# Sampled attention stream: one copy per bank of turned weights, exponentials in four portions

## The chip, the cores and the metric

The kernel runs on one core of a Trainium2 chip. A core has a matrix engine, TensorE (PE in the profile), which reads from the on-chip memory SBUF and writes to the accumulator banks of PSUM; VectorE (DVE), ScalarE (ACT) and GpSimd (POOL) for the rest of the arithmetic; and SyncE (SP), which issues most transfers. Each engine runs its own instructions strictly in order and waits for the others by semaphores. The metric is the time of one execution in device microseconds; less is better.

## The reference

The program is one inference step of a one-layer hybrid decoder. Two kinds of rows go through the same weights: a prompt of 2048 new tokens, and 8 sampled sequences of 8 new tokens each with 8192 cached positions. Half of the mixer is attention with forget gates (8 heads of 64), the other half an mLSTM matrix memory (4 heads of 128). An output projection, a layer norm, a squared-ReLU MLP (1024 to 4096 to 1024) and a second layer norm follow. The part that the change touches is the attention of the sampled sequences over their paged cache:

```python
s_past = jnp.einsum('bqhd,bkhd->bhqk', q, k_past).astype(jnp.float32) * scale
s_past = s_past + Ln[..., :, None] + R[:, :, None, :]
...
p = jax.nn.softmax(jnp.concatenate([s_past, s_new], axis=-1), axis=-1).astype(v_new.dtype)
o = jnp.einsum('bhqk,bkhd->bqhd', p[..., :P], v_past) + jnp.einsum('bhqk,bkhd->bqhd', p[..., P:], v_new)
```

All inputs and results are fp32. Large products are made as three products of rounded halves (lines 157 to 159: hi x hi, lo x hi, hi x lo), whose halves ScalarE (line 149, the hi part) and VectorE (line 152, the lo part) make from each weight or activation piece.

## The kernel before, in words

The main line of the program has four stages: A, the input projection with convolution, gates and mLSTM (to about 900 us, tiles `pm`, `whi`, `wlo`); B, the prompt's attention (to about 1325 us); O, the output projection and first norm (to about 1560 us, tiles `pw`, `y`, `px`, `x1h`, `x1l`); and C, the MLP in blocks of rows (tiles `ph`, `hq`, `h`, `py`), each block beginning with norms and transposes of its rows.

Beside it runs the sampled stream, `sample_attention` (line 1856), a generator that the main line advances one step at a time, paced by the estimated time of the matmuls recorded (`tick`, line 129). It has 295 steps n; a sequence b takes 32 of them and its stages overlap with those of the next:

- GpSimd gathers cached keys by indirect DMA into the ring `kT` (line 1996), VectorE turns them (line 2002), TensorE multiplies them with the query (`sQ`, line 2025), and VectorE adds the forget terms and takes running maxima (line 2032). A sequence's 8192 positions leave four pieces `S` (u = 0 to 3), each 128 x 2 x 512.
- At step 35 + 32b, `softmax` finds the maximum over everything (`m4`, line 2057) and ScalarE makes the exponentials in place, eight of 128x512 (line 2062) and two small ones for the new tokens (line 2064), each with its row sums in `rp`.
- At step 37 + 8u', `weights` turns piece u: for each half hg, TensorE makes four 128x128 transposes into one PSUM bank (`sT`, line 2094), which are copied out to `PTs` (line 2096), quarters 0 and 2 by VectorE, 1 and 3 by ScalarE. `sT` and `sQ` and the other small products of the stream share one bank (tag `sX`, one buffer), so the next of them waits until the bank has been emptied. That makes 64 banks of turned weights in all.
- `pv_step` multiplies `PTs` with gathered values (`sO`, line 2137), sixteen times per sequence; step 39 prepares the new tokens' weights (`softmax_new`), step 41 the reciprocal of the row sums (`softmax_sum`), step 70 closes the sequence.

The order on each engine is not the order of the code. The code records instructions; the framework's scheduler then places them by a simulated time line and by what each depends on (`schedule_with_timeline_sim`), and the stream's instructions are only kept behind the last ones of the main line (`beside`, line 114). So a change of one stage moves rows on all engines from there on.

Of the kernel before, what the change touches and what calls it, by code (L numbers as in the profile page):

```python
# [10 lines left out]
F32 = mybir.dt.float32  # L11
F32R = mybir.dt.float32r
I32 = mybir.dt.int32
AF = mybir.ActivationFunctionType
OP = mybir.AluOpType
AX = mybir.AxisListType
# [1839 lines left out]
def sample_attention(tc, I, O, ps_, pps, cst, ident, sqk, dnl, dR, dmix, dqb, vx, kx, pe, ring_a):  # L1856

    nc = tc.nc
    V, A, G, T, SY = nc.vector, nc.scalar, nc.gpsimd, nc.tensor, nc.sync
# [81 lines left out]
    for g in range(2):  # L1941
        p = pps.tile([32, 8, 64], F32, name="sT", tag="sX", bufs=1)
# [16 lines left out]
    state = {}  # L1959
# [9 lines left out]
    def q_load(b):  # L1969
        qt = ps_.tile([128, 2, 16, 8], F32, name="qt", bufs=2)  # L1970
        for n in range(2):
            SY.dma_start(qt[:, n].rearrange("p d t -> p (d t)"), dap(dqb, (n * NB + b) * 4096, [[0, 4], [128, 32], [1, 128]]))
        bn = ps_.tile([128, 2, 8], F32, name="bn", bufs=2)
        for hg in range(2):
            SY.dma_start(bn[:, hg], dap(dnl, hg * 4 * TOT + S + b * 8, [[TOT, 4], [0, 32], [1, 8]]))
        state[b] = dict(qt=qt, bn=bn, U=[])
# [21 lines left out]
    def k_turn(n):  # L1998

        for i in range(2):  # L2000
            x = piece(n)[:, i * 512:(i + 1) * 512]
            V.transpose(x, x)  # L2002
# [34 lines left out]
    def softmax(b):  # L2037
        z = state[b]
        pq = pps.tile([128, 2, 256], F32, name="sQ", tag="sX", bufs=1)
        for hg in range(2):  # L2040
            for db in range(2):
                for h4 in range(4):
                    hd = (hg * 4 + h4) * 2 + db
                    T.matmul(pq[h4 * 32:h4 * 32 + 32, hg, 0:8], z["qb"][:, hd], z["kr"][:, hd],
                             start=(db == 0), stop=(db == 1), skip_group_check=True)
        for hg in range(2):
            V.tensor_tensor_reduce(out=z["Sn"][:, hg], in0=pq[:, hg, 0:8], in1=z["bn"][:, hg], scale=1.0, scalar=NEG,
                                   op0=OP.add, op1=OP.max, accum_out=z["mx"][:, hg, 16:17])

        V.tensor_reduce(mt[:, 0:2], z["mx"], axis=AX.X, op=OP.max)  # L2050
        m2 = ps_.tile([128, 32], F32, name="m2", bufs=2)
        V.transpose(m2, mt)
        m3 = ps_.tile([128, 8], F32, name="m3", bufs=2)
        V.tensor_reduce(m3, m2.rearrange("p (g q) -> p q g", q=8), axis=AX.X, op=OP.max, negate=True)
        V.tensor_copy(m2.rearrange("p (g q) -> p g q", q=8), m3[:, None, :].to_broadcast([128, 4, 8]))
        m4 = ps_.tile([128, 32], F32, name="m4", bufs=2)
        V.transpose(m4, m2)
        rp = z["rp"] = ps_.tile([128, 2, 5], F32, name="rp", bufs=2)
        for u in range(4):
            for hg in range(2):  # L2060
                x = z["U"][u][:, hg].rearrange("p b k t -> p (b k t)")
                A.activation(x, x, AF.Exp, bias=m4[:, hg:hg + 1], accum_out=rp[:, hg, u:u + 1])
        for hg in range(2):
            A.activation(z["Sn"][:, hg], z["Sn"][:, hg], AF.Exp, bias=m4[:, hg:hg + 1], accum_out=rp[:, hg, 4:5])

    def softmax_new(b):

        z = state[b]
        rs = z["rs"] = ps_.tile([128, 2], F32, name="rs", bufs=2)
        V.tensor_reduce(rs, z["rp"], axis=AX.X, op=OP.add)  # L2070
        pn = z["pn"] = ps_.tile([8, 2, 32], F32, name="PTn", bufs=2)
        p = pps.tile([8, 2, 128], F32, name="sT", tag="sX", bufs=1)
        for hg in range(2):
            T.transpose(p[:, hg], z["Sn"][:, hg], ident)
        for hg in range(2):
            A.copy(pn[:, hg].rearrange("p (h q) -> p h q", q=8), p[:, hg].rearrange("p (h g q) -> p g h q", g=4, q=8)[:, 0])

    def softmax_sum(b):
        z = state[b]
        pl = pps.tile([128, 1], F32, name="sT", tag="sX", bufs=1)  # L2080
        for hg in range(2):
            T.matmul(pl, sel[:, hg].rearrange("p a b -> p (a b)"), z["rs"][:, hg:hg + 1], start=(hg == 0), stop=(hg == 1))
        rl = z["rl"] = ps_.tile([128, 1], F32, name="rl", bufs=2)
        V.reciprocal(rl, pl)

    def weights(b, u, hg):

        z = state[b]
        if hg == 0:
            z["PT"] = ps_.tile([128, 2, 4, 4, 4, 8], F32, name="PTs", tag="PTs", bufs=1)  # L2090
        PT = z["PT"]
        p = pps.tile([128, 4, 128], F32, name="sT", tag="sX", bufs=1)
        for f in range(4):
            T.transpose(p[:, f], z["U"][u][:, hg, f].rearrange("p k t -> p (k t)"), ident)
        for f in range(4):
            (A.copy if f % 2 else V.tensor_copy)(PT[:, hg, f].rearrange("p g h q -> p h g q"),
                                                 p[:, f].rearrange("p (h g q) -> p h g q", g=4, q=8))

    def v_new(b):
        vn = state[b]["vn"] = ps_.tile([8, 512], F32, name="vns", bufs=1)  # L2100
        SY.dma_start(vn, O["v_sample"][0, b].rearrange("t h d -> t (h d)"))
# [15 lines left out]
    def v_room():  # L2117
        return kx["free"] and vx["next"] < 128 and len(vx["live"]) < (2 if vx["more"] else 1) and (0 not in vx["live"] or vx["more"])
# [30 lines left out]
    def pv_end(b):  # L2149
        z = state.pop(b)  # L2150
        p = pps.tile([128, 2, 128], F32, name="sT", tag="sX", bufs=1)
        for c in range(2):
            T.transpose(p[:, c], z["os"][:, c * 128:(c + 1) * 128], ident)
        for hh in range(2):
            s = slice(hh * 64, hh * 64 + 64)
            for c in range(2):
                for hg in range(2):
                    V.tensor_reduce(mixs[s, hg * 2 + c, b * 8:b * 8 + 8],
                                    p[s, c].rearrange("p (e g h q) -> p g h q e", e=2, g=2, q=8)[:, hg, 2 * c + hh],
                                    axis=AX.X, op=OP.add)  # L2160

    def at(n, first, of):

        i, r = divmod(n - first, of)
        return i if r == 0 and i >= 0 else None
# [4 lines left out]
    def step(n):  # L2170
        after = None
        if n == 0:
            q_load(0)
        g, r = divmod(n - 2, 4)
        if 0 <= g < GA and r >= 2:
            k_turn(4 * g + 2 * r - 4)
            k_turn(4 * g + 2 * r - 3)
        if NA + 2 < n < 260:
            for i in turns.pop(n, ()):
                k_turn(i)  # L2180
        g = at(n, 6, 4)
        if g is not None and g < 64:
            after = qk_step(g)
        b = at(n, 35, 32)
        if b is not None and b < 8:
            softmax(b)
        due = (n - 38) // 2 if n > NA + 2 else (n - 39) // 2
        lead = 2
        while done[0] < 128 and done[0] - (lead == 1 and done[0] % 2) <= due and got.get(done[0], n) <= n - lead:
            after = pv_step(done[0] // 16, done[0] % 16, after)  # L2190
            done[0] += 1
            lead = 1
        b = at(n, 70, 32)
        if b is not None:
            pv_end(b)
        b = at(n, 39, 32)
        if b is not None and b < 8:
            softmax_new(b)
            v_new(b)
        b = at(n, 41, 32)  # L2200
        if b is not None and b < 8:
            softmax_sum(b)
        u = at(n, 37, 8)
        if u is not None and u < 32:
            for hg in range(2):
                weights(u // 4, u % 4, hg)
        b = at(n, 30, 32)
        if b is not None and b < 7:
            q_load(b + 1)
        b = at(n, 3, 32)  # L2210
        if b is not None and b < 8:
            q_begin(b)
        g = at(n, 4, 4)
        if g is not None and g < 64:
            r_load(g)
        if n >= 35 and (n % 2 == 1 or not vx["live"]):
            while v_room():
                got[vx["next"]] = n
                v_gather()
        g, r = divmod(n - 2, 4)  # L2220
        if 0 <= g < GA and r < 2:
            k_gather(4 * g + 2 * r, r == 1)
            k_gather(4 * g + 2 * r + 1, r == 1)
        if NA + 6 <= n < 256 and n % 4 != 3:
            k_gather(n, r >= 2)
            if n % 4 == 2:
                k_gather(n + 1)
# [38 lines left out]
```

## Time and profile before

| | |
|---|---|
| median of 3 runs | 3270.63 us (3259.38 to 3270.8) |
| profiled execution, time and span | 3264.98 us, 3263.1 us |
| PE busy | 3174.9 us (97%) |
| DVE busy | 2230.5 us (68%) |
| ACT busy | 1393.6 us (43%) |
| POOL busy | 1049.9 us (32%) |
| mean granted TensorE clock | 0.99 |

A group's row gives an engine, a line, an operation with its tile, and after the bar the busy time and the mean duration. A row of waits reads "who waited <- for whom: us in total, times, longest". A timeline row begins with start and duration in us; in brackets stands how long the engine was idle before it and what ended that. In a row of the windows each engine has its busy time and instruction count (PE, PEld, DVE, ACT, POOL), and then come the granted TensorE clock, the share of the DMA engines and GB/s.

### The profile page before, as it was taken

Reading aid. Unit: us, or ns where it says so; the run is one execution under the profiler, and the core shown is the slowest. Engines: PE = TensorE matmul, PEld = TensorE weight load, DVE = VectorE, ACT = ScalarE, POOL = GpSimd, SP = SyncE. Lnnn points to the kernel's source line nnn. Section 1 sums busy time; section 2 is a strip of 40 time slices with the busy share of each in tenths; the row PEclk is TensorE's granted clock in tenths of the full one; section 3 lists DMA queues with packets and bytes.
Section 4 is the critical chain, followed back from the end, with each engine's and each line's share of the span. In section 5 each row is a group of like instructions: output and inputs, shape, how many; then the busy total and the mean of one; then the engine's idle time right before and its main releaser. Section 6 shows DMA issues by size and latency. Waiting matters only on the chain.

```text
span 3263.1 us, 54920 instructions
## 1 busy us (share of the span) xinstructions
PE 3174.9 (97%) x20140; PEld 2555.0 (78%) x20140; DVE 2230.5 (68%) x5239; ACT 1393.6 (43%) x2753; POOL 1049.9 (32%) x1171
## 2 busy tenths in 40 slices
PE   9999999999999999999999999999999999999998
PEld 8878787786777777777777777777777777799997
DVE  5857667666577777766566767666667545777777
ACT  4444244444377777412333333242423333454443
POOL 0011121432344444354333324323234210264441
PEclk9999999999999999999999999999999999999999
DMA  6565774977743224777686768776678645442221
GB/s 193 150 198 167 231 230 144 315 259 218 222 128 85 79 84 118 254 282 263 250 289 213 288 238 288 263 249 244 239 240 305 210 160 176 134 139 84 91 90 56
DMA packets 413845, 641.88 MB, mean 197 GB/s; under 512 B 83020, under 2 KB 295312, under 8 KB 412680
## 3 DMA queue, kind: packets, MB, share of 16 engines
q1 hardware_dynamic: 337320, 360.99, 36.4%
q0 software_dynamic: 74304, 270.57, 22.3%
q10 hardware_dynamic: 1952, 6.82, 0.6%
q8 instruction: 159, 2.61, 0.3%
q14 instruction: 110, 0.90, 0.1%
HBM read 585.43 MB, written 52.83 MB: 196 GB/s over the span
## 4 chain that ended last, share of the span: by engine, by line
PE 60%; DMA 5%; DVE 3%; issue 2%; POOL 1%; ACT 1%; SPq 0%; DVEq 0%; POOLq 0%; ACTq 0%
PE ph L157 7%; PE ph L158 7%; PE ph L159 7%; PE py L157 6%; PE py L159 6%; PE py L158 6%; PE po L1245 4%; PE pt L1228 4%; PE sO L2137 3%; PE pS L1187 2%; PE sQ L2025 2%; PE pS L1188 2%; DMA kT<-cache_k,idxK 2%; DMA xr<-cache_v,idxV 1%; PE pw L158 1%
## 5 line engine op out<-in xcount | busy, mean ns | idle before, releaser
L149 ACT ACTIVATE wh<-wr 128x1024 fp32r<-128x1024 f32 x268 | 277.6, 1056 | 538.2 <-PE py L159 299.8
L1996 POOL DMA_INDIRECT kT<-cache_k,idxK x256 | 262.3, 1025 | 741.1 <-PE sQ L2025 644.1
L2002 DVE STREAM_TRANSPOSE kT<-kT 128x512 f32<-128x512 f32 x512 | 330.2, 686 | 230.2 <-DMA kT<-cache_k,idxK 229.5
L157 PE MATMUL ph<-x1h,wh 128*128 128x512 f32 (+2 forms) x1280 | 453.5, 354 | 3.1 <-ACT xr L1664 2.1
L159 PE MATMUL ph<-x1h,wl 128*128 128x512 f32 (+2 forms) x1280 | 450.7, 354 | 6.0 <-DVE wl L152 6.0
L158 PE MATMUL ph<-x1l,wh 128*128 128x512 f32 (+2 forms) x1280 | 452.9, 354 | 0.0
L152 DVE TENSOR_TENSOR wl<-wr,wh 128x1024 fp32r<-128x1024 f32 x252 | 318.7, 1272 | 77.9 <-PE ph L159 45.8
L157 PE MATMUL py<-wh,h 128*128 128x512 f32 (+1 forms) x888 | 347.7, 395 | 0.8 <-DVE y L1807 0.3
L159 PE MATMUL py<-wh,h 128*128 128x512 f32 (+1 forms) x888 | 347.7, 392 | 0.0
L158 PE MATMUL py<-wl,h 128*128 128x512 f32 (+1 forms) x888 | 347.5, 392 | 0.0
L1607 DVE TENSOR_TENSOR y<-y,py 128x512 f32<-128x512 f32 x336 | 224.2, 677 | 142.6 <-PE py L159 140.6
L159 PEld LDWEIGHTS ph<-x1h,wl 128*128 128x128 f32 x1280 | 242.0, 189 | 38.9 <-DVE wl L152 7.1
L157 PEld LDWEIGHTS ph<-x1h,wh 128*128 128x128 f32 x1280 | 242.3, 189 | 38.1 <-ACT xr L1664 2.3
L158 PEld LDWEIGHTS ph<-x1l,wh 128*128 128x128 f32 x1280 | 242.1, 189 | 35.1 <-issue 2.5
L2113 POOL DMA_INDIRECT vt<-cache_v,idxV x156 | 160.6, 1030 | 291.0 <-PE sO L2137 252.1
L157 PE MATMUL pm<-whi,xhT 128*128 128x512 f32 (+2 forms) x648 | 235.7, 365 | 3.7 <-ACT acb L637 1.5
L158 PE MATMUL pm<-wlo,xhT 128*128 128x512 f32 (+2 forms) x648 | 230.7, 356 | 1.9 <-DVE wlo L152 1.9
L159 PE MATMUL pm<-whi,xlT 128*128 128x512 f32 (+2 forms) x648 | 230.6, 356 | 0.0
L157 PEld LDWEIGHTS py<-wh,h 128*128 128x128 f32 x888 | 167.1, 188 | 42.9 <-issue 7.8
L159 PEld LDWEIGHTS py<-wh,h 128*128 128x128 f32 x888 | 167.1, 188 | 36.2 <-issue 2.5
L158 PEld LDWEIGHTS py<-wl,h 128*128 128x128 f32 x888 | 167.1, 188 | 33.8 <-issue 2.9
L149 ACT ACTIVATE whi<-wra 128x1024 fp32r<-128x1024 f32 (+1 forms) x112 | 119.0, 1062 | 160.7 <-PE pm L159 105.6
(485 smaller groups left out, 7068.4 us busy)
## 6 DMA issues: line engine op xcount, KB each, us to landing
wr<-w SPq DMA_DIRECT2D x256, 512.0 KB
wra<-w_in SPq DMA_DIRECT2D x112, 512.0 KB
Rb<-dR SPq DMA_DIRECT2D x128, 128.0 KB
wr<-w_o SPq DMA_DIRECT2D x16, 512.0 KB
xr<-dmix SPq DMA_DIRECT2D x16, 512.0 KB
y<-x_prompt SPq DMA_DIRECT2D x16, 512.0 KB
dx<-y SPq DMA_DIRECT2D x16, 512.0 KB
qn<-dq SPq DMA_DIRECT2D x120, 64.0 KB
```

The source lines that it names most:

```text
L149: last["ACT"] = A.activation(dst, src, AF.Copy, scale=scale)
L152: r = (eng or V).tensor_tensor(dst, src, hi.bitcast(F32), op=OP.subtract)
L157: T.matmul(ps, wh, xh, start=first, stop=False, skip_group_check=free)
L158: T.matmul(ps, wh, xl, start=False, stop=False, skip_group_check=free)
L159: last["PE"] = T.matmul(ps, wl, xh, start=False, stop=stop, skip_group_check=free)
L1228: T.transpose(pt[:, k], sc[i][0][k0 // 8][:, (k0 % 8 + k) * 128:(k0 % 8 + k + 1) * 128], ident)
L1245: last["PE"] = T.matmul(po[c:c + 64, q0:], z["vn"][:, k], PTs[k // 4][:, k % 4, q0:], start=k == same[0], stop=k == same[-1], skip_group_c ...
L1607: V.tensor_tensor(y, y, ps, op=OP.add)
L1996: G.indirect_dma_start(out=piece(n), out_offset=None, in_=ck, in_offset=IO(ap=idxK[:, b, j // 2, j % 2:j % 2 + 1], axis=0))
L2002: V.transpose(x, x)
L2113: vx["last"] = G.indirect_dma_start(out=vt.rearrange("p f c -> p (f c)"), out_offset=None, in_=cv, in_offset=IO(ap=idxV[:, b, (kt % 4) * 4 ...
L2137: after_ = T.matmul(po[r:r + 32], z["PT"][:, hg, 2 * f + g, pg].rearrange("p h q -> p (h q)"), vts[f][:, g, hg * 256:(hg + 1) * 256], star ...
```

## The change

Two things are changed, both in the sampled stream.

In `weights`, the four copies of a bank become one copy of 128x512 by ScalarE (line 2098 after the change). VectorE no longer takes part in emptying the bank.

The exponentials leave `softmax` and become a function of their own, `exps`, called in four portions: piece u's two at step 36 + 32b + u, so one to four steps after the maximum, the small ones of the new tokens with the first portion. The reduction of the row sums (`rs`) moves from `softmax_new` at step 39 to step 40, one step ahead of the product that uses it.

```diff
-        for u in range(4):
+        z["m4"] = m4
+
+    def exps(b, u):
+
+        z = state[b]
+        for hg in range(2):
+            x = z["U"][u][:, hg].rearrange("p b k t -> p (b k t)")
+            A.activation(x, x, AF.Exp, bias=z["m4"][:, hg:hg + 1], accum_out=z["rp"][:, hg, u:u + 1])
+        if u == 0:
             for hg in range(2):
-                x = z["U"][u][:, hg].rearrange("p b k t -> p (b k t)")
-                A.activation(x, x, AF.Exp, bias=m4[:, hg:hg + 1], accum_out=rp[:, hg, u:u + 1])
-        for hg in range(2):
-            A.activation(z["Sn"][:, hg], z["Sn"][:, hg], AF.Exp, bias=m4[:, hg:hg + 1], accum_out=rp[:, hg, 4:5])
+                A.activation(z["Sn"][:, hg], z["Sn"][:, hg], AF.Exp, bias=z["m4"][:, hg:hg + 1], accum_out=z["rp"][:, hg, 4:5])
...
     def softmax_new(b):
...
-        rs = z["rs"] = ps_.tile([128, 2], F32, name="rs", bufs=2)
-        V.tensor_reduce(rs, z["rp"], axis=AX.X, op=OP.add)
...
         for f in range(4):
             T.transpose(p[:, f], z["U"][u][:, hg, f].rearrange("p k t -> p (k t)"), ident)
-        for f in range(4):
-            (A.copy if f % 2 else V.tensor_copy)(PT[:, hg, f].rearrange("p g h q -> p h g q"),
-                                                 p[:, f].rearrange("p (h g q) -> p h g q", g=4, q=8))
+        A.copy(PT[:, hg].rearrange("p f g h q -> p f h g q"), p.rearrange("p f (h g q) -> p f h g q", g=4, q=8))
...
         if b is not None and b < 8:
             softmax(b)
+        b, u = divmod(n - 36, 32)
+        if 0 <= b < 8 and u < 4:
+            exps(b, u)
...
+        b = at(n, 40, 32)
+        if b is not None and b < 8:
+            z = state[b]
+            z["rs"] = ps_.tile([128, 2], F32, name="rs", bufs=2)
+            V.tensor_reduce(z["rs"], z["rp"], axis=AX.X, op=OP.add)
```

The scheduler places everything anew from the first turned piece on. Two places show it; the prediction calls them A and O. **Place A** is sequence 0's first piece in stage A. On TensorE (`sT` transposes, `sO` value products, `pm` the main line), the rows are the same up to this piece of the difference:

```order
 L158 MATMUL pm<-wlo,xhT 128x512
 L159 MATMUL pm<-whi,xlT 128x512
-L2137 MATMUL sO<-vt,PTs 32x256
+L2097 MATMUL sT<-ident,S 128x128 x4
+L2138 MATMUL sO<-vt,PTs 32x256
 L157 MATMUL pm<-whi,xhT 128x512
 L158 MATMUL pm<-wlo,xhT 128x512
```

The transposes of the second half now stand where the first value product stood; before they came some twenty matmul rows later. ScalarE at the same place before (`L2062` and `L2064` exponentials; `L844`, `L851`, `L856` gates of the mLSTM; `L643` and `L637` convolution):

```order
L2062 ACTIVATE S,rp<-S,m_5623 128x512 x8
L2064 ACTIVATE Sn,rp<-Sn,m_5623 128x8 x2
L653 ACTIVATE qi<-acb 128x512
L647 COPY hist<-qi 128x3
L149 ACTIVATE whi<-wra 128x1024
L653 ACTIVATE qi<-acb 128x512
L844 ACTIVATE gsb<-gsb 128x16
L851 ACTIVATE Wm<-Wm,gm 128x128 x2
L2096 COPY PTs<-sT 128x4x4x8
L851 ACTIVATE Wm<-Wm,gm 128x128 x2
L856 ACTIVATE qa<-qa 128x512
L859 ACTIVATE den<-gm 128x4
```

and after the change, from the last three exponentials on:

```order
L2066 ACTIVATE S,rp<-S,m_5623 128x512 x3
L149 ACTIVATE whi<-wra 128x1024
L844 ACTIVATE gsb<-gsb 128x16
L851 ACTIVATE Wm<-Wm,gm 128x128 x2
L653 ACTIVATE qi<-acb 128x512
L851 ACTIVATE Wm<-Wm,gm 128x128
L2098 COPY PTs<-sT 128x4x4x4x8
L851 ACTIVATE Wm<-Wm,gm 128x128
L856 ACTIVATE qa<-qa 128x512
L626 COPY qi<-hist 128x3
L643 COPY qi<-pm 128x512
L637 ACTIVATE acb<-pm,cw 128x512
```

ScalarE's part of emptying the bank stands behind `L844` in both; one `L653` and one `L851` more stand between now. **Place O** is the end of the output projection. TensorE before (`px` transposes of rows `xr` and `y`, `sQ` key products):

```order
L2094 MATMUL sT<-ident,S 128x128 x4
L1403 MATMUL px<-ident,xr 128x128 x8
L1403 MATMUL px<-ident,y 128x128 x8
L2025 MATMUL sQ<-kT,qb 32x256 x16
L2137 MATMUL sO<-vt,PTs 32x256 x8
L157 MATMUL ph<-x1h,wh 128x512
```

and after:

```order
L2097 MATMUL sT<-ident,S 128x128 x4
L157 MATMUL pw<-wh,mh 128x512
L158 MATMUL pw<-wl,mh 128x512
L159 MATMUL pw<-wh,ml 128x512
L157 MATMUL pw<-wh,mh 128x512
L158 MATMUL pw<-wl,mh 128x512
L159 MATMUL pw<-wh,ml 128x512
L1403 MATMUL px<-ident,xr 128x128 x8
L2025 MATMUL sQ<-kT,qb 32x256 x16
L2138 MATMUL sO<-vt,PTs 32x256 x8
L1403 MATMUL px<-ident,y 128x128 x8
L157 MATMUL ph<-x1h,wh 128x512
```

The second half's transposes stand six projection rows earlier, and `sQ` and `sO` ahead of the transposes of `y`. ScalarE there before (`x1h` the hi half of the turned rows, `L175` a row's scaling in its norm, `wh` a weight piece):

```order
L149 ACTIVATE x1h<-px 128x4x128 x3
L2096 COPY PTs<-sT 128x4x4x8
L149 ACTIVATE x1h<-px 128x4x128
L149 ACTIVATE wh<-wr 128x1024
L2096 COPY PTs<-sT 128x4x4x8
L175 ACTIVATE y<-y,ln 128x1024
L149 ACTIVATE x1h<-px 128x4x128
L2096 COPY PTs<-sT 128x4x4x8
L149 ACTIVATE x1h<-px 128x4x128
L149 ACTIVATE wh<-wr 128x1024 x2
L2096 COPY PTs<-sT 128x4x4x8
L149 ACTIVATE x1h<-px 128x4x128 x2
```

and after:

```order
L149 ACTIVATE x1h<-px 128x4x128 x2
L2098 COPY PTs<-sT 128x4x4x4x8
L149 ACTIVATE x1h<-px 128x4x128 x2
L149 ACTIVATE wh<-wr 128x1024
L2098 COPY PTs<-sT 128x4x4x4x8
L175 ACTIVATE y<-y,ln 128x1024
L149 ACTIVATE wh<-wr 128x1024
L149 ACTIVATE x1h<-px 128x4x128 x2
L149 ACTIVATE wh<-wr 128x1024
L149 ACTIVATE x1h<-px 128x4x128 x2
L149 ACTIVATE wh<-wr 128x1024
L175 ACTIVATE y<-y,ln 128x1024
```

Both halves' copies now stand ahead of the first `L175`; before, two of the four quarters that ScalarE took stood behind it.

## The prediction

> **What bounds the kernel now.** I read the page's head first, then the waits (all engines, then TensorE's own), then the timeline where a wait on TensorE's list names the tiles that the change touches.
>
> ```profile
> span 3263.1 us, 54920 instructions
> ...
> PE 3174.9 (97%) x20140; PEld 2555.0 (78%) x20140; DVE 2230.5 (68%) x5239; ACT 1393.6 (43%) x2753; POOL 1049.9 (32%) x1171
> ```
>
> TensorE (PE) is busy for all but 88.2 us, so a change that takes no matmul away can win only what lies in that idle time and in stretches at a reduced clock. This change leaves all matmuls and transposes as they are. ACT and DVE have room: work moved between them is free unless it makes TensorE wait.
>
> ```profile
> ACT PTs L2096 <- DVE PTs L2096: 215.3, 92, 11.0
> ```
>
> That is the target: ScalarE's copies out of the transposes' bank waited 215.3 us in 92 stops for VectorE's copy from the same bank. But what did TensorE lose by it? Its own list of waits:
>
> ```profile
> PE px L1403 <- DMA xr<-dx: 6.4, 2, 5.6
> PE ph L159 <- DVE wl L152: 6.0, 3, 3.0
> ...
> PE px L1403 <- DVE x1l L152: 4.9, 1, 4.9
> ...
> PE pm L157 <- ACT acb L637: 4.4, 2, 2.9
> ...
> PE sO L2137 <- DVE PTs L2096: 2.8, 1, 2.8
> ...
> PE sT L2094 <- ACT PTs L2096: 2.0, 1, 2.0
> ...
> PE sQ L2025 <- ACT PTs L2096: 1.7, 1, 1.7
> ...
> PE ph L157 <- ACT wh L149: 1.0, 1, 1.0
> ```
>
> Only three rows name PTs, 6.5 us in three stops out of 64 half pieces. The timeline puts the three at two places, each with a neighbouring wait that the same copies cause in part. The 215.3 us are thus almost wholly ScalarE's own idle time.
>
> **Place A** is sequence 0's first piece, at 548 us, still in the first stage:
>
> ```profile
> 550.00 0.22 ACT L844 ACTIVATE gsb<-gsb 128x16 f32<-128x16 f32 x1 [4.90 <-DMA gsb<-dgs]
> 550.12 0.68 ACT L851 ACTIVATE Wm<-Wm,gm 128x128 f32<-128x128 f32 x2
> 550.70 0.24 ACT L2096 COPY PTs<-sT 128x128 f32<-128x128 f32 x1
> ...
> 550.98 0.29 DVE L2096 COPY PTs<-sT 128x128 f32<-128x128 f32 x1 [4.54 <-ACT PTs L2096]
> ...
> 551.32 0.62 PE L2137 MATMUL sO<-vt,PTs 128*32 128x256 f32 x2 [2.84 <-DVE PTs L2096]
> 551.44 0.62 ACT L856 ACTIVATE qa<-qa 128x512 f32<-128x512 f32 x1
> ...
> 552.06 0.18 ACT L626 COPY qi<-hist 128x3 f32<-128x3 f32 x1
> ...
> 552.14 0.58 ACT L643 COPY qi<-pm 128x512 f32<-128x512 f32 x1
> 552.62 0.78 ACT L637 ACTIVATE acb<-pm,cw 128x512 f32<-128x512 f32 x1
> ...
> 553.45 0.80 PE L157 MATMUL pm<-whi,xhT 128*128 128x512 f32 x1 [1.51 <-ACT acb L637]
> ```
>
> ScalarE stands in L844 until a DMA lands at 550.00; the copy of the second quarter is queued behind it, VectorE's third quarter behind that, TensorE behind both. The real releaser is the DMA, not the two-engine chain.
>
> **Place O** is the end of the output projection, at 1545 us (sequence 2's second piece):
>
> ```profile
> 1544.80 0.27 ACT L2096 COPY PTs<-sT 128x128 f32<-128x128 f32 x1 [4.98 <-DVE PTs L2096]
> ...
> 1547.11 0.66 PE L2094 MATMUL sT<-ident,S 128*128 128x128 f32 x4 [2.00 <-ACT PTs L2096]
> ...
> 1550.39 1.24 ACT L175 ACTIVATE y<-y,ln 128x1024 f32<-128x1024 f32 x1 [3.34 <-DVE ln L174]
> ...
> 1553.55 1.98 PE L1403 MATMUL px<-ident,y 128*128 128x128 f32 x8 [4.91 <-DVE x1l L152]
> ...
> 1555.96 1.06 ACT L149 ACTIVATE wh<-wr 128x1024 fp32r<-128x1024 f32 x1 [2.24 <-DMA wr<-w]
> ...
> 1557.07 1.09 ACT L149 ACTIVATE x1h<-px 128x512 fp32r<-128x512 f32 x2
> ...
> 1557.22 3.64 PE L2025 MATMUL sQ<-kT,qb 128*32 128x256 f32 x32 [1.69 <-ACT PTs L2096]
> ...
> 1560.77 1.04 ACT L149 ACTIVATE wh<-wr 128x1024 fp32r<-128x1024 f32 x1
> ```
>
> After the first stop the big one, 4.91, hangs on x1l, whose x1h stands on ScalarE behind L175, the scaling of a normed row (3.34 us of wait for VectorE's statistics); then comes a weight DMA (2.24). The windows give the clock that such stops cost:
>
> ```profile
> 548.49:553.45 4.96, 0.62 (x3) 0.14 (x3) 0.31 (x2) 3.46 (x13) 1.26 (x1) 0.87 0.75 278
> 553.45:560.00 6.55, 6.55 (x17) 5.24 (x18) 5.89 (x8) 2.89 (x9) 0.66 (x1) 0.58 0.11 39
> ...
> 1545.10:1562.50 17.40, 8.80 (x70) 4.91 (x69) 15.03 (x33) 9.38 (x14) 6.33 (x6) 0.71 0.73 259
> ```
>
> The seventh column is the granted clock. At A, 4.34 us idle, then 6.55 us at 0.58, a loss of 0.42 x 6.55 = 2.8: 7.1 in all. At O 8.6 us idle; 0.29 x 17.4 = 5.0 us of full clock are taken away, partly from idle time; TensorE's 8.80 busy us less some 1.6 of transposes at 1547 to 1549 ran at half speed, 7.2 x 0.5 = 3.6 lost: 12.2. Both together 19.3 us, which bounds what the copies can give back.
>
> The Trainium skill, "TensorE: Matmul & The Clock Gate", section "Part 1: The HAM clock gate", has the array at half rate after an idle window of about 3.4 us. The trace has it halve after 2.84 and 1.51 us with 0.62 us of work between, so it trips a little earlier here. By the page a single longer stop at A would be gated, and by the row it is gated now: the term below is the same by either.
>
> **The change part by part.** Durations of the parts:
>
> ```profile
> L2096 DVE COPY PTs<-sT x128: 233/283/293, 540.3 to 2725.5; 128x128 f32<-128x128 f32 x128
> L2096 ACT COPY PTs<-sT x128: 238/266/285, 550.7 to 2725.8; 128x128 f32<-128x128 f32 x128
> ...
> L2062 ACT ACTIVATE S<-S,m x64: 706/709/731, 536.7 to 2568.6; 128x512 f32<-128x512 f32 x64
> ...
> L643 ACT COPY qi<-pm x40: 345/569/595, 53.7 to 765.6; 128x512 f32<-128x512 f32 x24, 128x256 f32<-128x256 f32 x16
> ```
>
> *Engine time.* VectorE loses 128 x 0.283 = 36.2 us. ScalarE loses 128 x 0.266 = 34.0 and gains 64 copies of 128x512; the nearest row is L643, same shape and also out of PSUM, 0.58 us: 37.1. So ScalarE grows by 3 us, hidden (43% busy). The new copy writes in pieces of eight floats, which L643 does not; L2096 writes so too and at 0.266 for a quarter shows no dearer fixed part, so between 0.58 and 4 x 0.266 = 1.06 I take 0.58. Even 1.06 adds 31 us to ScalarE and delays a bank by 0.5 us.
>
> *Exponentials.* The eight of a sequence, 8 x 0.709 = 5.7 us, stood in one run on ScalarE. They now stand in up to four runs; in sequence 0 there are only two short rows between, from sequence 2 on mostly three or four runs with other work between. Their cover is ScalarE's idle time, before and after; no row of TensorE's waits names L2062, and the one for wh, which could stand behind it, is 1.0 us. Worth 0; if the cover failed, one run of 5.7 us behind a weight split would be the price of each of 8 sequences. The row sums move to step 40, one step ahead of their matmul; VectorE waits there only for exponentials one step old. 0.
>
> *Place A after the change.* TensorE's order is the same up to the stop, except that the second half's four transposes now stand where the first sO did, so it arrives at the same 548.49. Its releaser is the whole first copy, which stands behind L844 (ends 550.22), two L851 (550.80), L653 (0.62, as L856: 551.4), one L851 (551.75), then 0.58: 552.3. The next wait, for L637, follows as before: 552.3 plus L851 0.34, L856 0.62, L626 0.18, L643 0.58, L637 0.78 = 554.8, against 553.40 now. That is 1.4 later, with 0.4 us of transposes done meanwhile: **+1.0**. Bounds: -7.1 (the DMA comes earlier) and +3 (a second gated stretch). What is late next is L157 and its convolution chain.
>
> *Place O after the change.* ScalarE copies at about 1539.4 instead of being held to 1544.8, so the 2.00 goes; sQ and sO are moved ahead of the y transposes, so the 1.69 goes too. But the chain L174, L175, x1h, x1l remains between the px transposes, and its L175 comes only about half a microsecond sooner (two copies of 0.28 leave VectorE ahead of it). Then wh waits for the same DMA: 1555.96 + 1.06 = 1557.0, two x1h 1558.1, the next wh 1559.1, which no longer has the second L175 ahead of it. TensorE's ph can start about 1559.2 instead of 1562.50. Of these 3.3 us part runs at half clock: **-2.5**, bounds -12.2 and 0.
>
> *Other waits on VectorE.* With 36 us less in its queue a late wl comes by at most two copies (0.57 us) sooner; three such stops in the second row of the list: -1.7 to 0, I take **-0.5**.
>
> *Order.* The scheduler has rewritten most of TensorE's order (12,934 rows against 12,919), which shifts gathers and block edges by microseconds either way; I have no sign for it: 0, with the size of the largest DMA stop, 5.6 us, and its clock as the spread.
>
> Sum: the profiled execution took 3264.98 us (span 3263.1 and 1.9 around it); 3264.98 + 1.0 - 2.5 - 0.5 = **3263 us**. That is 0.23% below the median of the three runs, 3270.63, which themselves span 3259.38 to 3270.8.
>
> **The rivals.** *Both places clear* (0.22). If at A the landing or the order on ScalarE turns out earlier and at O the 4.98 us by which ScalarE was held was the root of the whole stop, all 19.3 us go: 3245.7. For it: the hold ends just before the stop. Against: L844's DMA and L175's statistics are in the chain anyway.
>
> *The one copy holds the bank* (0.14, slower). The same bank serves sT and sQ. Near the block edges ScalarE has an in-order wait such as
>
> ```profile
> 1982.44 1.25 ACT L175 ACTIVATE y<-y,ln 128x1024 f32<-128x1024 f32 x1 [8.80 <-DVE ln L174]
> ```
>
> and in the new order a second-half copy stands right behind this L175, while sQ follows its transposes after only some 29 matmul rows, 6.6 us at the 0.23 us between the starts of
>
> ```profile
> 1539.69 0.40 PE L158 MATMUL pw<-wl,mh 128*128 128x512 f32 x1
> ...
> 1539.92 0.40 PE L159 MATMUL pw<-wh,ml 128*128 128x512 f32 x1
> ```
>
> Before, half the quarters went through VectorE and the halves stood further apart. Price of one edge: 8.80 + 1.25 + 0.58 - 6.6 = 4.0 us idle and as much again in the gated stretch, 5, so 9. With three edges inside the stream 27: 3292. It decides from the point where a copy comes over 6.6 us after its transposes; by the present times it comes at about that point, which is why I give it weight.
>
> *The portions do not separate* (0.08): the scheduler puts them next to each other again and the copies change nothing at O: 3265.
>
> **How the numbers follow.** My forecast has 0.56, with its own range of 3252 to 3276 (place A and O bounds taken in part, and one DMA stop of 5.6 us either way). What a measurement of this kernel can tell from no change is about 0.5%, 16 us. Faster by more: the first rival, and a little of the forecast's lower end, 0.25. Slower by more: the second rival, 0.14. Within: 0.61. The range reaches to the first rival's 3246 and most of the way to the second's: 3246 to 3285.
>
> **What would show it.** Right: the ACT PTs row with DVE as its releaser is gone, TensorE's busy time stays within 10 us of 3175, a stop of about 3.9 us before the second sT at 548 with a gated stretch behind it, ph starting after the projection some 3 us sooner. Wrong: no stop at 548; sQ or sT waiting on ACT PTs at a block edge (second rival); DVE busy not down by some 36 us; or a stop at another place over 6 us, which would be the order's doing.

## The result, and the profile after

The changed kernel takes 3258.98 us (median of 22 runs, 3252.13 to 3269.25), the kernel before on the same chip 3265.82 us (22 runs, 3259.38 to 3276.28). The ratio is 0.9978, with a 95% interval of 0.9970 to 0.9987: 0.2% faster, and inside the half per cent within which I called it the same. The profiled execution takes 3255.96 us (3254.1 of span) against 3264.98, so it is 9.0 us shorter.

The head of the page after, and the new copy's and the exponentials' lines (duration in ns: least, median, most):

```profile
span 3254.1 us, 54648 instructions
...
PE 3174.1 (98%) x20140; PEld 2555.5 (79%) x20140; DVE 2196.9 (68%) x5111; ACT 1398.1 (43%) x2689; POOL 1049.1 (32%) x1171
```

```profile
L2098 ACT COPY PTs<-sT x64: 559/580/598, 552.8 to 2712.9; 128x512 f32<-128x512 f32 x64
...
L2066 ACT ACTIVATE S<-S,m x64: 706/710/734, 538.4 to 2566.8; 128x512 f32<-128x512 f32 x64
```

TensorE is as busy as before (3174.1 against 3174.9 us); VectorE has lost 33.6 us and ScalarE gained 4.5. The waits after, first the row of ScalarE's copy, then TensorE's own list:

```profile
ACT PTs L2098 <- PE sT L2097: 98.1, 25, 9.6
```

```profile
PE sO L2138 <- DMA vt<-cache_v,idxV: 11.7, 3, 4.6
...
PE ph L159 <- DVE wl L152: 3.4, 2, 2.9
PE px L1403 <- DVE x1l L152: 3.3, 1, 3.3
PE sT L2097 <- ACT PTs L2098: 3.2, 1, 3.2
```

The wait of 215.3 us of ScalarE for VectorE is gone. Its copies now wait 98.1 us, and for TensorE, whose transposes fill the bank. On TensorE another row leads: value products `sO` that wait for gathered values, 11.7 us. Before, the same row stood third:

```profile
PE sO L2137 <- DMA vt<-cache_v,idxV: 5.8, 3, 4.2
```

**Where the 9.0 us are.** I compared the start of the same matmul (the nth of its line and tile, main line only) in both traces and took the median difference over each 50 us. Positive means that the program after runs later:

| stretch, us | after minus before, us | what lies there |
|---|---|---|
| 500 to 550 | +3.0 | the two are the same program up to here: scatter of one execution |
| 550 to 600 | +2.8 | place A is passed |
| 900 to 1300 | +8.1 | stops at 640, 687 and 764 us |
| 1540 to 1550 | +2.7 | projection |
| 1560 to 1600 | -1.9 | place O is passed |
| 1950 to 2000 | -2.8 | just ahead of a block's edge |
| 2050 to 2100 | -10.4 | two stops of a block's edge are gone |
| end | -9.0 | |

Counted from the +3.0, the small net is a sum of larger terms: -0.2 at A, +5.3 in the rest of stage A, -5.4 from there to 1540, -4.6 at O, -7.6 at one edge, +0.5 elsewhere: -12.0. This is one pair of executions; the medians are 6.8 us apart.

**Place A** in the timeline after, and its windows (columns as before, the seventh the clock):

```profile
551.30 0.22 ACT L844 ACTIVATE gsb<-gsb 128x16 f32<-128x16 f32 x1 [5.00 <-DMA gsb<-dgs]
...
552.81 0.56 ACT L2098 COPY PTs<-sT 128x512 f32<-128x512 f32 x1
...
553.43 1.11 PE L2097 MATMUL sT<-ident,S 128*128 128x128 f32 x4 [3.24 <-ACT PTs L2098]
...
555.50 0.80 PE L157 MATMUL pm<-whi,xhT 128*128 128x512 f32 x1
```

```profile
550.19:553.43 3.24, 0.00 (x1) 0.00 (x1) 0.69 (x1) 2.13 (x7) 0.00 (x0) 0.95 0.92 338
553.43:560.00 6.57, 6.57 (x17) 4.43 (x18) 4.45 (x6) 4.74 (x14) 1.90 (x2) 0.51 0.20 75
```

One stop of 3.24 us where there were 2.84 and 1.51, and the clock behind it at 0.51 instead of 0.58. The last main-line matmul ahead of the stop is 1.7 us later than before, the first behind it 2.05 us and those behind the slow stretch 1.6 us, so the place as a whole costs next to nothing. The +3.0 had become 1.7 already at 546 us: before, TensorE waited there 0.24 and 0.53 us for the two halves of a weight piece, and after, coming later, it does not.

**Place O** before, four rows of VectorE that the prediction did not show, then the same place after (`L1453` adds a product to the row `y`, ahead of its statistics):

```profile
1542.63 1.30 DVE L2002 STREAM_TRANSPOSE kT<-kT 128x512 f32<-128x512 f32 x2 [2.68 <-DMA kT<-cache_k,idxK]
...
1543.86 0.65 DVE L1453 SCALAR_TENSOR_TENSOR y<-y,pw 128x512 f32<-128x512 f32 x1
...
1544.43 0.28 DVE L2096 COPY PTs<-sT 128x128 f32<-128x128 f32 x1
...
1550.14 0.21 DVE L174 TENSOR_SCALAR ln<-ln 128x1 f32<-128x1 f32 x1 [0.47 <-POOL ln L173]
```

```profile
1537.03 2.48 DVE L2002 STREAM_TRANSPOSE kT<-kT 128x512 f32<-128x512 f32 x4
...
1541.09 0.69 DVE L1453 SCALAR_TENSOR_TENSOR y<-y,pw 128x512 f32<-128x512 f32 x1 [1.58 <-PE pw L159]
...
1541.52 0.59 ACT L2098 COPY PTs<-sT 128x512 f32<-128x512 f32 x1 [5.24 <-PE sT L2097]
...
1546.60 0.21 DVE L174 TENSOR_SCALAR ln<-ln 128x1 f32<-128x1 f32 x1
...
1546.97 0.59 ACT L2098 COPY PTs<-sT 128x512 f32<-128x512 f32 x1 [2.12 <-PE sT L2097]
...
1547.45 1.24 ACT L175 ACTIVATE y<-y,ln 128x1024 f32<-128x1024 f32 x1
...
1550.50 1.06 ACT L149 ACTIVATE wh<-wr 128x1024 fp32r<-128x1024 f32 x1 [1.81 <-DMA wr<-w]
...
1551.59 2.95 DVE L152 TENSOR_TENSOR wl<-wr,wh 128x1024 fp32r<-128x1024 f32 x1 [0.80 <-ACT wh L149]
...
1554.47 1.27 DVE L152 TENSOR_TENSOR x1l<-px,x1h 128x512 fp32r<-128x512 f32 x2
...
1555.20 1.25 PE L1403 MATMUL px<-ident,y 128*128 128x128 f32 x8 [3.27 <-DVE x1l L152]
...
1556.54 0.76 PE L157 MATMUL ph<-x1h,wh 128*128 128x512 f32 x1
```

```profile
1545.10:1562.50 17.40, 12.83 (x91) 8.95 (x90) 11.80 (x23) 7.54 (x10) 11.66 (x9) 0.83 0.75 245
```

Before, VectorE waited 2.68 us for a gather ahead of its transposes of keys. Behind them stood both its addition to `y`, from which the statistics follow, and its copy of the bank; ScalarE's next quarter (4.98 us of wait) stood behind the copy, and ScalarE's `x1h` behind that quarter. After, ScalarE empties the bank by itself, and the transposes of keys are through before the projection's rows end, so the addition to `y` waits for TensorE alone (1.58 us). The statistics are done at 1546.60, although the program is 2.7 us later by then, and L175 no longer waits. What is left of TensorE's stop, 3.27 us, hangs on a weight piece: ScalarE's `wh` waits for its DMA, VectorE's `wl` for `wh`, and `x1l` stands behind `wl`.

**The stops that moved**, one row of the timeline after and two of before:

```profile
768.04 1.47 PE L2138 MATMUL sO<-vt,PTs 128*32 128x256 f32 x12 [4.09 <-DMA vt<-cache_v,idxV]
```

```profile
1992.65 0.80 PE L159 MATMUL ph<-x1h,wl 128*128 128x512 f32 x1 [2.54 <-DVE wl L152]
...
2024.90 1.45 PE L2025 MATMUL sQ<-kT,qb 128*32 128x256 f32 x21 [1.86 <-issue]
```

The first is new: before, one such stop stood at 797.68 us (4.19 us), and after there is one at 806.25 us (3.06 us) as well. The other two have gone. Between 1960 and 2030 us TensorE idled 5.7 us before, and not at all after.

### The profile page after: what moved, and what is told of

Its sections match the earlier page's. It is cut to its first block, busy times and chain, and to the rows that moved or that the text cites. A ratio compares the mean times of both kernels' runs of the same rounds, so it can differ in the third digit from the quotient of the medians.

```text
span 3254.1 us, 54648 instructions
## 1 busy us (share of the span) xinstructions
PE 3174.1 (98%) x20140; PEld 2555.5 (79%) x20140; DVE 2196.9 (68%) x5111; ACT 1398.1 (43%) x2689; POOL 1049.1 (32%) x1171
## 3 DMA queue, kind: packets, MB, share of 16 engines
q1 hardware_dynamic: 337320, 360.99, 36.2%
## 4 chain that ended last, share of the span: by engine, by line
PE 79%; DMA 7%; DVE 6%; issue 5%; POOL 1%; ACT 1%; SPq 0%; DVEq 0%; POOLq 0%; ACTq 0%
PE ph L159 6%; PE ph L157 6%; PE ph L158 6%; PE py L157 6%; PE py L158 5%; PE py L159 5%; PE pm L157 5%; PE pm L158 5%; PE pm L159 5%; PE po L1245 4%; PE pt L1228 4%; DMA kT<-cache_k,idxK 3%; PE sQ L2025 3%; PE sO L2138 3%; PE pS L1187 2%
## 5 line engine op out<-in xcount | busy, mean ns | idle before, releaser
L152 DVE TENSOR_TENSOR wlo<-wra,whi 128x1024 fp32r<-128x1024 f32 (+1 forms) x112 | 137.6, 1229 | 81.5 <-ACT whi L149 81.0
```

The lines of the kernel that those rows point to most:

```text
L152: r = (eng or V).tensor_tensor(dst, src, hi.bitcast(F32), op=OP.subtract)
```

## The experiments

Three theories stood at the start. T1: the copy part carries the gain, since ScalarE is no longer held by VectorE's copies. T2: any edit makes the scheduler lay the order anew, and the stops fall otherwise whatever the edit is. T3: the portions carry it.

Twelve measurements were made in three groups of four, each group on a chip of its own and against runs of the kernel before on that chip. The kernel before takes 3339.51, 3340.56 and 3348.47 us there, 2.3 to 2.5% more than in the first comparison. All versions compute the whole output. The ratios and intervals are the recorded estimates; they can differ from the quotient of the two medians by a tenth of a per cent. Results:

| version | group | us | ratio to before | 95% interval |
|---|---|---|---|---|
| copy part alone | 1 | 3346.71 | 1.0011 | 0.9988 to 1.0035 |
| portions alone | 1 | 3344.55 (one execution of 4495.88 is not in the ratio) | 1.0007 | 0.9986 to 1.0029 |
| row sums one step later, alone | 1 | 3342.73 | 0.9999 | 0.9970 to 1.0028 |
| change, copy by VectorE | 1 | 3323.86 | 0.9950 | 0.9931 to 0.9970 |
| the change itself | 2 | 3347.62 | 1.0016 | 0.9997 to 1.0036 |
| copy by VectorE, no portions | 2 | 3333.13 | 0.9983 | 0.9963 to 1.0003 |
| change, four copies, all ScalarE | 2 | 3348.38 | 1.0014 | 0.9993 to 1.0036 |
| change, copy by VectorE, again | 2 | 3317.07 | 0.9926 | 0.9899 to 0.9952 |
| kernel before, as a control | 3 | 3342.95 | 0.9992 | 0.9975 to 1.0009 |
| VectorE early, ScalarE late | 3 | 3343.01 | 0.9987 | 0.9968 to 1.0006 |
| ScalarE early, VectorE late | 3 | 3322.92 | 0.9922 | 0.9896 to 0.9949 |
| change, copy by VectorE, third | 3 | 3324.88 | 0.9927 | 0.9907 to 0.9947 |

The control differs from 1 by 0.0008, with an interval of 0.0017 to either side. A change of 0.2% is at the limit of what one group can tell.

### One part at a time

The copy part alone is the change without the edits to the exponentials and row sums; the portions alone keep the four copies. The order control moves nothing but the row sums:

```diff
-        rs = z["rs"] = ps_.tile([128, 2], F32, name="rs", bufs=2)
-        V.tensor_reduce(rs, z["rp"], axis=AX.X, op=OP.add)
...
+        b = at(n, 40, 32)
+        if b is not None and b < 8:
+            z = state[b]
+            z["rs"] = ps_.tile([128, 2], F32, name="rs", bufs=2)
+            V.tensor_reduce(z["rs"], z["rp"], axis=AX.X, op=OP.add)
```

> The one copy by ScalarE alone, the exponentials and the row sums as before. Theory 1 (ScalarE is no longer held by VectorE's copies): this part carries the gain, ratio to before 0.997 to 0.999, the stop at the end of the output projection (17.4 us for 1545 to 1562 before) shorter by 5 us or more, no row ACT PTs <- DVE PTs. Theory 2 (the scheduler's new order moves stops about, whatever the edit): ratio anywhere in 0.995 to 1.005, with no relation to the copies. Theory 3 (the portions carry the gain): ratio 0.999 to 1.001.

> The four portions and the later row sums alone, four copies by two engines as before. Theory 1: no gain, ratio 0.999 to 1.002, ACT PTs <- DVE PTs still near 215 us. Theory 2: 0.995 to 1.005. Theory 3: 0.997 to 0.999.

> Only the reduction of the row sums moves from step 39 to step 40: eight VectorE instructions of 0.16 us, which cost nothing by themselves. A measure of what a rewritten order does alone. Theories 1 and 3: 0.9995 to 1.0005. Theory 2: the time moves by 3 us or more either way (below 0.999 or above 1.001), with stops of TensorE at other places.

None of the three can be told from 1, so no part alone carries a gain there. Their traces still say which part moves which stop. Two rows of the copy part alone, then one of the portions alone:

```profile
770.98 1.07 PE L2135 MATMUL sO<-vt,PTs 128*32 128x256 f32 x16 [3.61 <-DMA vt<-cache_v,idxV]
```

```profile
1564.42 1.95 PE L1403 MATMUL px<-ident,y 128*128 128x128 f32 x8 [3.27 <-DVE x1l L152]
```

```profile
1554.76 1.12 PE L1403 MATMUL px<-ident,y 128*128 128x128 f32 x4 [4.91 <-DVE x1l L152]
```

The copy part brings the shorter stop at O (3.27 as after, 4.91 with the portions alone as before), and it also brings the stop for values near 764 us. The portions and the row sums alone show neither, and keep ScalarE's wait for VectorE's copies (202.6 and 201.2 us). So the gain at O and that loss in stage A come as a pair from the same edit: T1 is right on the place, T2 wrong for these two stops, T3 without support. The pair belongs to emptying a bank by one engine, whichever that is: with VectorE making the one copy in all banks, the stop near 767 us (2.0 to 5.1 us in four traces) and the missing 4.91 us at O are there too. How the edit shortens O is read from the timeline: in the traces of the kernel before, the portions alone and the row sums alone, VectorE waits 2.1 to 2.8 us for keys ahead of its addition to `y`. In the copy part alone and the change it does not. The copy by VectorE without portions still has this wait (2.60 us), and its stops at O sum to 5.5 us, against 8.6 before and 4.5 after; so the wait for keys is only a part of it.

### The change again, and the copy by the other engine

```diff
-        A.copy(PT[:, hg].rearrange("p f g h q -> p f h g q"), ...)
+        V.tensor_copy(PT[:, hg].rearrange("p f g h q -> p f h g q"), ...)
```

> All of the change, but the one copy is made by VectorE (128x512) and not by ScalarE. If what counts is that a bank is emptied by one engine in one piece (theory 1 in its general form): 0.997 to 0.999, as the change. If what counts is that VectorE is relieved of 36 us and its queue of norms and weight halves: 1.000 or slower, to 1.004, with sQ or sT waiting on DVE PTs at block edges. Theory 2: 0.995 to 1.005 without such a pattern.

> The changed kernel once more, so that the versions beside it are compared with it on one chip. Theory T1 (the copy part moves the stops: it clears those between 1544 and 1570 us and adds one near 764 us; its sum is a gain of some 7 us) expects 0.9965 to 0.999 of the kernel before. Rival T4 (the 7 us seen at first belong to how the stops fell on that chip and do not carry over, as copies and portions alone gave 1.0011 and 1.0007 on a second chip) expects 0.999 to 1.003. In the trace both expect one stop of about 3.3 us ahead of the first px in the window 1545 to 1565 us, and a stop of 3 to 4 us of sO on the landing of vt near 764 us.

> The changed kernel with its one copy by VectorE, run again beside the changed kernel. If its 0.995 came from VectorE taking the 0.58 us copies off ScalarE (ScalarE busy about 33 us less than in the changed kernel, so that its hi parts of the weights come earlier in the stretch from 1600 us on), it is ahead of the changed kernel again, by 0.2 to 0.6 per cent, and its stops 'py <- y' and 'py/ph <- wl' in that stretch sum to 5 us or more less. If the lead was only of the other chip's slower stretch from 1600 to 2550 us, the two are within 0.15 per cent wherever that stretch is not slower.

The change measured 1.0016 here, against 0.9978 at first, and the intervals do not overlap: the first theory (T1, a gain of some 7 us that carries over) missed, its rival T4 held. Both stops are where they were at first:

```profile
767.46 1.93 PE L2138 MATMUL sO<-vt,PTs 128*32 128x256 f32 x16 [3.62 <-DMA vt<-cache_v,idxV]
```

```profile
1563.87 1.35 PE L1403 MATMUL px<-ident,y 128*128 128x128 f32 x8 [3.28 <-DVE x1l L152]
```

Compared matmul by matmul with the kernel before in group 3, the change is 1.1 us later at 500 us, 11.3 later at 900, 2.8 earlier at 1700, and 1.0 earlier at the end. It loses some 10 us by the end of stage A, where it had lost 5 at first, and wins some 14 us between 1500 and 1700, where it had won 5, but wins nothing net after that. The two profiles here come from two chips, so a microsecond or two of this is not to be relied on.

The copy by VectorE, which I had tried as an undoing of ScalarE's part, was faster than the kernel before on three chips (0.995, 0.9926 and 0.9927; the first lies outside the ranges of both theories about the copy), and faster than the change on the one chip where both ran. It is 0.9% ahead of the change in group 2, where I had asked for 0.2 to 0.6. Between 1600 and 2550 us its rows for `y` and `wl` (py <- y, ph <- wl, py <- wl) sum to 16.5 + 4.3 + 0.8 = 21.6 us, those of the change to 18.8 + 4.5 + 2.2 = 25.5: the sign is as expected, but it is 3.9 us where I had asked for 5 or more, and explains little of the 29 us by which the two traces differ at the end. The larger of these rows, with the copy by VectorE and in the change:

```profile
PE py L157 <- DVE y L1607: 16.5, 12, 3.6
```

```profile
PE py L157 <- DVE y L1607: 18.8, 16, 2.6
```

### Number and length of the copies, and the portions

```diff
-        A.copy(PT[:, hg].rearrange("p f g h q -> p f h g q"), ...)
+        for f in range(4):
+            A.copy(PT[:, hg, f].rearrange("p g h q -> p h g q"), p[:, f].rearrange("p (h g q) -> p h g q", g=4, q=8))
```

> The changed kernel, but each bank left in four copies of one piece each, all by ScalarE: 256 copies of about 0.27 us in place of 64 of 0.58 us, some 31 us more of ScalarE, and no copy of a bank waits for the other engine. The theory 'it is the wait of one engine for the other that the change takes away' expects the stops of the changed kernel and 0.997 to 1.000 of the kernel before, with sT waiting up to 0.5 us longer per second bank. The rival 'it is the number and length of the copies' expects no gain or a loss, 1.000 to 1.005, since a bank is held for about 1.07 us rather than 0.58.

> The kernel before with one copy per bank, by VectorE alone, and the exponentials as they were. T1 in the form 'one engine per bank is what counts, whichever it is' expects most of what the version with portions gave (0.995): 0.994 to 0.998, and the window 1545 to 1565 us as in the changed kernel (one stop of about 3 us). The rival 'portions and the VectorE copy only together' expects 0.999 to 1.002. In both, ScalarE is busy about 33 us less than in the changed kernel (64 copies of 0.58 us less, 0.06 us each for the rest) and VectorE about 6 to 8 us more than in the kernel before less 36 us plus 43.5 us.

Four copies by ScalarE hold a bank longer:

```profile
L2099 ACT COPY PTs<-sT x256: 238/272/341, 552.4 to 2803.8; 128x128 f32<-128x128 f32 x128
```

That is 4 x 0.272 = 1.09 us against 0.58, and the time is the same, 1.0014 beside 1.0016. By the bounds as I had written them it counts for the rival that number and length matter; beside the change itself, though, it shows that they cost nothing that can be measured (the intervals are some 0.2% to either side, 7 us). The copy by VectorE without the portions gives 0.9983, with them 0.9926 on the same chip, intervals apart. So portions are worth about half a per cent when VectorE copies, and nothing that shows when ScalarE does (1.0011 without, 1.0016 with, on two chips). Neither theory had that; nor does the first theory's one stop of about 3 us at O appear, but three of 1.4, 2.4 and 1.3 us. Why is open: the trace puts 11.1 us between these two versions, 6 of them after 2300 us, and no one stop accounts for it.

### Which copies make VectorE's version faster

```diff
-        A.copy(PT[:, hg].rearrange("p f g h q -> p f h g q"), ...)
+        (V.tensor_copy if b >= 2 else A.copy)(PT[:, hg].rearrange("p f g h q -> p f h g q"), ...)
```

This is ScalarE early, VectorE late; the other has `b < 2` and covers stage A and the projection up to 1445 us.

> The kernel before itself, as a level for the three beside it and for its own stops where the program runs near 3340 us. Both theories expect a ratio of 0.998 to 1.002. If the longer time on the other chips belongs to the chip and not to a version, its trace shows the same 60 to 90 us between 1550 and 2550 us as the versions, and no more than 5 us of it in a stop that the change touches (sT or sQ waiting for PTs, sO waiting for vt).

> The changed kernel with its copy by VectorE for the first two sequences (16 banks, up to 1445 us) and by ScalarE for the other six. Theory T5 (the lead of the VectorE copy over the ScalarE copy is made from 1545 us on, where the copies of ScalarE stand ahead of its hi parts of the weights: the run with one copy by VectorE was 4 us ahead of the changed kernel at 1400 us and 29 us at the end) expects 0.9995 to 1.003 of the kernel before. Rival T6 (the first two sequences set how everything later falls) expects 0.992 to 0.996, as with one copy by VectorE throughout.

> The reverse: ScalarE copies the 16 banks of the first two sequences, VectorE the 48 of the other six. T5 expects 0.993 to 0.997 of the kernel before, T6 0.9995 to 1.003.

> One copy by VectorE throughout, a third time, beside the two halves of it: 0.992 to 0.996 of the kernel before if it is a property of the program wherever the kernel before needs about 3340 us; 0.996 to 0.999, near the 0.9978 of the changed kernel, on a chip where the kernel before needs about 3266 us.

T5 held and T6 fell: with VectorE late 0.9922, as with VectorE throughout (0.9927 beside it); with VectorE early 0.9987, not to be told from 1 and short of what T6 asked. Both are a tenth of a per cent faster than the numbers I had set for T5. So, with the portions in place, the lead is made by the 48 late copies. The matmuls of the two half versions are 5.5 us apart at 1550 us in favour of VectorE early, and 27.5 us apart at the end in favour of VectorE late. The groups of waits between 1545 and 2550 us, first with ScalarE late, then with VectorE late:

```profile
DVE h L152 <- ACT h L149: 30.3, 21, 4.6
```

```profile
PE py L157 <- DVE y L1607: 29.9, 20, 5.4
```

```profile
DVE h L152 <- ACT h L149: 17.4, 15, 3.7
```

```profile
PE py L157 <- DVE y L1607: 15.9, 11, 3.6
```

With ScalarE copying, VectorE waits 13 us more for ScalarE's hi half of `h`, and the accumulation `y` is queued behind that on VectorE; TensorE waits 14 us more for `y`. The windows of the same stretch, ScalarE late, then VectorE late:

```profile
1545.00:2550.00 1005.00, 939.18 (x5804) 714.62 (x5803) 604.49 (x1151) 325.98 (x495) 315.32 (x316) 0.97 0.69 240
```

```profile
1545.00:2550.00 1005.00, 960.65 (x6000) 733.02 (x5999) 654.72 (x1227) 317.38 (x472) 324.36 (x325) 0.98 0.70 247
```

TensorE gets through 6000 instead of 5804 matmuls in that time. That the engine of the late copies makes the difference is shown by the edit, since nothing else differs in the source. That it does so through the copy's place in ScalarE's queue is not shown: the edit also lays the order on all engines anew, the chain h, y, py is read from the waits and was not tested by itself, and in group 2 the same `py <- y` row differs by 2.3 us only. Nor does the chain explain the lead over the kernel before, whose `py <- y` row is only 9.2 us. The version with VectorE copying was not run on a chip where the kernel before takes 3266 us, so what it gives there is open.

## Why the prediction was right, and where it was not

The time came out inside the forecast: 3255.96 us for the profiled execution against 3263 with a range of 3252 to 3276, the median 0.2% below the kernel before. On another chip the answer was again "same". The terms with a sign, A, O and the late wl, were to give -2.0 us and gave about -7. The order, to which I had given no sign, moved single stretches by 5 us and more both ways; that these nearly cancelled is luck.

- **The target was mostly idle time of ScalarE's own.** Right. 215.3 us of waits went away and TensorE's stops moved by microseconds.
- **Engine time.** VectorE was to lose 36.2 us and lost 33.6; ScalarE was to gain 3 and gained 4.5. The row of L643 (0.58) was the right one for the copy: 0.580. The half microsecond by which four copies would delay a bank is worth nothing that can be measured, as four copies by ScalarE showed.
- **Place A, +1.0.** The step was right: the stop came, and its releaser is the first copy behind L844, L851, L653 and L851. The size was too large: I had forecast 3.9 us of stop and it is 3.24, with a gated stretch (reduced clock) behind it as before, and the place as a whole costs about 0 (from 1.7 to 1.6 us late). The Trainium skill, "TensorE: Matmul & The Clock Gate", section "Part 1: The HAM clock gate", puts the idle window at about 3.4 us; the windows above show 3.24 us without work followed by a clock of 0.51, so the gate again trips a little earlier than by the page.
- **Place O, -2.5.** That the hold of ScalarE goes was right, but the term was too small: it measured -4.6. The step that failed is "its L175 comes only about half a microsecond sooner", and with it that the norm's chain remains what the stop hangs on. L174 comes 3.5 us sooner by the clock (1546.60 against 1550.14). I had taken two copies off VectorE ahead of the statistics, and from the addition to `y` to L174 it does take 0.8 us less (5.51 against 6.28). The other 2.8 us I had overlooked: the addition itself (1541.09 against 1543.86) stood behind VectorE's wait for a key gather, and no longer does. L175 then waits for nothing, and the stop that is left hangs on the weight DMA and `wl`.
- **Order, 0.** This is the term that was really mis-sized. In the first pair of traces the program lost 5.3 us in stage A, and won 5.4 before O and 7.6 at the edge at 2000 us. I had allowed one stop of 5.6 us either way; there were three stretches of that size, and the first two cancelled. The largest new stop, 4.6 us, is under the 6 us that I had named as a sign against me.
- **Late wl, -0.5.** The row fell from 6.0 to 3.4 us, so it is 2.6. Nearly all of it is the one stop of 2.54 us at the edge at 2000 us, which is gone whole; that a late wl comes half a microsecond sooner at each stop is not seen.
- **Exponentials, 0.** Right as far as seen: alone they measured 1.0007, and no row of TensorE's waits names them. That they matter once VectorE copies was not foreseen.
- **The rivals.** Both places did not clear. The bank is held behind a normed row at no edge after: the only wait of `sT` or `sQ` for the copy is the 3.2 us at A. In the trace of the change on the other chip `sT` waits for the copy once more, 3.1 us at about 2250. ScalarE stood idle ahead of that copy, so it is not the wait behind a normed row to which that rival had given 9 us an edge; what released the copy, that trace does not show.

That the change is worth 0.2% is a fact of the first comparison alone. Of its terms, the gain at O and the loss in stage A came back elsewhere; the one at the edge at 2000 us did not.

## What to carry to other kernels

A long wait between two helper engines is no time lost until a row of the busiest engine names it: here 215 us gave 7. Where a scheduler rewrites the order, an edit brings along gains and losses elsewhere, here of 5 to 8 us, so a gain of 0.2% should be measured on a second chip before it is kept. And before work is taken off an engine because that engine is busier, measure it on both: the same copy was better on VectorE, at 68% busy, than on ScalarE, at 43%. The waits suggest that this is because VectorE stands waiting for ScalarE's results.

## What the runs showed that I had not expected

The kernel before takes 2.3 to 2.5% longer in the three later groups than in the first comparison, and all of it between 1545 and about 2600 us, in the MLP beside the stream. The windows of the kernel before there, at first and in group 3:

```profile
1545.00:2550.00 1005.00, 980.87 (x6264) 756.92 (x6264) 677.66 (x1322) 348.13 (x565) 344.28 (x337) 0.99 0.73 257
```

```profile
1545.00:2550.00 1005.00, 939.62 (x5797) 713.75 (x5796) 629.75 (x1229) 323.59 (x531) 311.44 (x315) 0.97 0.68 240
```

TensorE idles 65 us instead of 24 and its clock is 0.97 instead of 0.99; up to 1545 us the two agree within some 2 us. The waits that name a tile of the change are hardly longer: sT and sQ for PTs and sO for vt sum to 5.4 us against 4.7, while rows with no visible releaser lead the list:

```profile
PE sQ L2044 <- issue: 16.1, 24, 1.2
```

Whether that belongs to these chips or to their condition at the time, and what it is, is open. Their traces lack some of the semaphores' records, so that waits are put down to "remote" there, and no run was made to settle it.
